# Two early weight blocks and an earlier residual in a two-block transformer kernel

## The chip, the cores and the metric

One core of a Trainium2 chip runs the kernel. TensorE (PE) multiplies, VectorE (DVE), ScalarE (ACT) and GpSimd (POOL) do the elementwise work, and SyncE (SP) issues most of the DMAs. The metric is the device time in microseconds of one execution, the median of several.

## The reference, cut to what matters

Two transformer blocks follow one another on 256 tokens of width 1024, in fp32. The first block (two layers, with attention, MLP and a final RMS norm) ends in `x`. The second block has two layers of its own, and each of them is this, with three attentions between (cut):

```python
for l in range(DEPTH):
    mod = jax.nn.silu(c) @ w_ada[l] + b_ada[l]
    shift, scale, gate = jnp.split(mod, 3, axis=-1)
    h = x * (1.0 + scale[:, None, :]) + shift[:, None, :]
    (p_cq, p_ckv, p_kr, p_qb, p_kb, p_vb, p_qc, p_kc, p_vc,
     p_qi, p_ki, p_wi, p_gate) = jnp.split(h @ w_in[l], SPLIT_POINTS, axis=-1)
    cq = rms_norm(p_cq, q_norm_g[l])        # 768 latents
    ckv = rms_norm(p_ckv, kv_norm_g[l])     # 256 latents
    ...
    sub = y @ w_out[l]
    x = layer_norm(ALPHA * x + (1.0 + gate[:, None, :]) * sub, ln_g[l], ln_b[l])
```

The term `ALPHA * x` is the residual that the change moves, and the 1024 latents are the columns whose weights it takes in early.

## The kernel before

The 256 tokens lie in two tiles of 128, "token 0" and "token 1" below (`t`). Every fp32 product is made of three matmuls: both factors are split into a rounded part (`whi`, `ahi`) and the rest (`wlo`, `alo`), and `mm3` (L330 to L332) adds hi x hi, lo x hi and hi x lo. Weights are streamed in blocks of 128 x 1024 by the class `Weights`, in the order of one list, `weight_plan`: SyncE loads a block into one of 4 raw buffers (L190, L194), ScalarE casts it to `whi` (L207), VectorE subtracts to `wlo` (L209). `get` hands out the next block of the list and keeps the split running two blocks ahead, in 5 buffers of each kind. `W.hold` ties later subtractions on VectorE behind a named instruction; `turn_input` sets it to the first alo.

The order on every engine is made by a scheduler from the program's order and its dependences. `tc.issue_after` adds an edge for instructions of the same engine.

The stages that the change touches:

- **End of the first block** (`mlp1`). The last four blocks (`m1w2`) give each token's sums; then per token come the RMS norm (L1238 to L1243, a pow on GpSimd in `rsqrt`, L340), two modulated halves (L1250), their transposes on TensorE (L1267), and the split of the transposed input into `ahi` (ScalarE, L1269) and `alo` (VectorE, L1270).
- **Entry of a layer of the second block** (`block2_layer`, `l` = 0 and 1). A loop takes steps for token 0, and three steps behind (`LAG`) the same steps for token 1. Its blocks are eight of the latents ("b2c", two halves of 512 columns with four blocks each), four of 392 columns ("b2vb") and two of 256 ("b2vc"). When a half is complete, VectorE multiplies it by the gains `lgain` (L1632), which SyncE loads (L1608, L1609). When both halves of a token are complete, `latent_scale` sums the squares, has GpSimd make the pow of two columns (L340), and scales the latents (L1645, L1646). Then they are transposed and split (L1667 to L1670).
- **The residual**, `resid`, ALPHA times the layer's input, needed at the layer's end. In layer 0 it is a product by a column (L1256) and one by a row (L1257) for each token, on GpSimd. In layer 1 it is two small products on GpSimd (L1881, L1882), a ScalarE activation (L1883), and two products or sums by a row on GpSimd (L1885), for each token.
- **End of a layer** (`out_tok`, `finish`): two halves of 512 columns for two tokens, with L1845 to L1847 on VectorE behind each, and for each token the layer norm (L1851 to L1859). Layer 0's end calls `turn_input` again; layer 1's stores the output (L1861).

Of the kernel before, what the change touches and what calls it, by code (L numbers as in the profile page):

```python
# [90 lines left out]
def weight_plan(A):  # L91
    plan = []

    def add(key, w, r0, nk, c0, nc_):
        plan.append((key, [(w[r0:r0 + 128 * nk, c0:c0 + nc_], 0, nc_)], nk, nc_))

    def group(key, w, c0, n=256):
        add(key + "0", w, 0, 4, c0, n)
        add(key + "1", w, 512, 4, c0, n)

    def mlp(l):
        w1, w2 = A["mlp_w1"][l], A["mlp_w2"][l]
        for e in range(9):
            if e < 8:
                for g in range(2):
                    group(f"m{l}w1", w1, e * 512 + g * 256)
            if e:
                for i in range(4):
                    if l:
                        add(f"m{l}w2", w2, e * 512 - 512 + 256 * (i // 2), 2, i % 2 * 512, 512)  # L110
                    else:
                        add(f"m{l}w2", w2, e * 512 - 512, 4, i * 256, 256)

    w = A["even_w_in"][0]
    for r0 in (0, 512):
        for c0 in (0, 256):
            add("l0in", w, r0, 4, c0, 256)
    for c0 in (512, 768, 1024, 1280):
        group("l0in", w, c0)
    w = A["even_w_out"][0]  # L120
    for kh in range(2):
        for g in range(4):
            add("l0out", w, kh * 512, 4, g * 256, 256)
    mlp(0)
    w = A["odd_w_in"][0]
    for kind, g in (("q", 0), ("q", 1), ("k", 0), ("v", 0), ("k", 1), ("v", 1),
                    ("q", 2), ("k", 2), ("v", 2), ("q", 3), ("k", 3), ("v", 3)):
        group("l1" + kind, w, {"q": 0, "k": 1024, "v": 2048}[kind] + g * 256)
    w = A["odd_w_out"][0]
    for kh in range(2):  # L130
        for g in range(4):
            add("l1out", w, kh * 512, 4, g * 256, 256)
    mlp(1)
    for l in range(2):
        w = A["w_in_2"][l]
        for g in range(2):
            for i in range(4):
                add("b2c", w, 256 * i, 2, 512 * g, 512)
        for i in range(4):
# [12 lines left out]
        for g in range(2):
            group("b2qi", w, 2976 + g * 256)
        one("b2qb", 1312)
        one("b2kb", 1696)
        add("b2uk", A["w_uk_2"][l], 0, 2, 0, 384)
        add("b2uv", A["w_uv_2"][l], 0, 2, 0, 384)
        for hh in range(2):
            for kq in range(3):

                r = A["w_uq_2"][l][256 * kq:256 * kq + 256, 288 * hh:288 * hh + 288]
                plan.append(("b2uq", [(r, a, n, c0) for a, n, c0 in ((0, 96, 0), (96, 16, 80), (112, 16, 64))], 2, 384))
        group("b2qc", w, 2208)
        group("b2kc", w, 2464)
        for g in (2, 1, 0, 3):
            group("b2g", w, 3560 + g * 256)
        for g in range(2):
            for i in range(4):
                add("b2o", A["w_out_2"][l], 256 * i, 2, 512 * g, 512)
    return plan  # L170


class Weights:
# [25 lines left out]
    def _split(self):  # L199
        i = self.i_split  # L200
        key, pieces, nk, n = self.plan[i]
        raw = self.raw.pop(i)
        hi = self.pool.tile([128, 1024], F32R, name="whi", tag="whi", bufs=self.bufs)
        lo = self.pool.tile([128, 1024], F32R, name="wlo", tag="wlo", bufs=self.bufs)
        m = nk * n
        with self.tc.issue_after(self.ahold) if self.ahold else contextlib.nullcontext():
            self.nc.scalar.copy(hi[:, :m], raw)  # L207
        with self.tc.issue_after(self.hold) if self.hold else contextlib.nullcontext():
            self.nc.vector.tensor_tensor(lo[:, :m], raw, hi[:, :m].bitcast(F32), op=OP.subtract)  # L209
        r = "p (k c) -> p k c"  # L210
        self.parts[i] = (hi[:, :m].rearrange(r, k=nk), lo[:, :m].rearrange(r, k=nk))
        self.i_split += 1
# [18 lines left out]
def cols(c, n=128):  # L231
    return slice(n * c, n * c + n)
# [48 lines left out]
class Net:  # L281
# [897 lines left out]
    def mlp1(self, a):  # L1179
# [25 lines left out]
        for e in range(8):  # L1205
# [16 lines left out]
            for i in range(4):  # L1222
                w = self.W.get("m1w2")
                for t in range(2):
                    product(e - 1, i, t, w)
            del hid[e - 1]
        ws = [self.W.get("m1w2") for _ in range(4)]
        hi4, lo4 = ([self.k4([128, 4, 256], F32R, name=n) for _ in range(2)] for n in ("ahi", "alo"))
        rstds = []
# [22 lines left out]
            rstds.append(rstd)  # L1252

        def resid(t, dep):
            with self.tc.issue_after(dep):
                nc.gpsimd.tensor_scalar(xt[t], xt[t], rstds[t], ALPHA, op0=OP.mult, op1=OP.mult)  # L1256
            nc.gpsimd.tensor_tensor(xt[t], xt[t], fr, op=OP.mult)  # L1257
            return xt[t]

# [2 lines left out]
    def turn_input(self, u, i, t, hi4, lo4):  # L1262

        nc = self.nc
        pt = self.psum("s" if i else "pt", [128, 4, 128])
        for k in range(4):
            nc.tensor.transpose(pt[:, k], u[:, cols(k)], self.ident)  # L1267
        hv, lv = (f[i][:, :, cols(t)] for f in (hi4, lo4))
        nc.scalar.copy(hv, pt)  # L1269
        op = nc.vector.tensor_tensor(lv, pt, hv.bitcast(F32), op=OP.subtract)  # L1270
        if i + t == 0:
            self.W.hold = op.ins


    def odd_q(self, wv, g, a):
# [324 lines left out]
    def block2_layer(self, l, a, resid):  # L1600
# [62 lines left out]
        for t in range(2):  # L1663
            for i in range(2):
# [3 lines left out]
                hv, lv = (f[i][:, :, cols(t)] for f in (chi4, clo4))  # L1668
                nc.scalar.copy(hv, pt)
                last = V.tensor_tensor(lv, pt, hv.bitcast(F32), op=OP.subtract)  # L1670
        xa = [resid(t, last.ins) for t in range(2)]
        last_lo = clo[7].bitcast(F32)


# [158 lines left out]
            hi4, lo4 = ([self.k4([128, 4, 256], F32R, name=n) for _ in range(2)] for n in ("ahi", "alo"))  # L1833
            hi, lo = ([t[:, i] for t in f for i in range(4)] for f in (hi4, lo4))
        mvs = []
        st = self.sb.tile([128, 2, 2, 6], F32, name="st", tag="st", bufs=1)

        def out_tok(g, t, ws):
            ps = self.psum("mm")
            for i, (wh, wl) in enumerate(ws):  # L1840
                for k in range(2):
                    kk = 2 * i + k
                    self.mm3(ps, (yh[kk][:, cols(t)], yl[kk][:, cols(t)]), (wh[:, k], wl[:, k]), kk == 0, kk == 7)
            c = cols(g, 512)
            V.tensor_tensor(z[t][:, c], ps, g1[:, c], op=OP.mult)  # L1845
            (V if g else nc.gpsimd).tensor_tensor(z[t][:, c], z[t][:, c], xa[t][:, c], op=OP.add)
            V.bn_stats(st[:, t, g], z[t][:, c])  # L1847

        def finish(t):
            mv = self.sm([128, 2])  # L1850
            V.bn_aggr(mv, st[:, t])  # L1851
            rstd = self.rsqrt(mv[:, 1:2], 1, 1.0, 1e-5, True)
            u = self.k4([128, 1024], name="u")
            for i in range(2):
# [9 lines left out]
            mvs.append((mv, rstd))  # L1864

        for g in range(2):
            ws = [self.W.get("b2o") for _ in range(4)]
            for t in range(2):
                out_tok(g, t, ws)
                if g:  # L1870
                    finish(t)
        if l == 1:
            return None, None
        def resid(t, dep):

            mv, rstd = mvs[t]
            r2, nb = self.sm([128, 1]), self.sm([128, 1])
            with self.tc.issue_after(dep):
                if t == 0:
                    nc.gpsimd.tensor_scalar(lnb, lnb, ALPHA, 0.0, op0=OP.mult, op1=OP.add)  # L1880
                nc.gpsimd.tensor_scalar(r2, rstd, ALPHA, 0.0, op0=OP.mult, op1=OP.add)  # L1881
            nc.gpsimd.tensor_scalar(nb, mv[:, 0:1], r2, -1.0, op0=OP.mult, op1=OP.mult)  # L1882
            nc.scalar.activation(z[t], z[t], AF.Identity, bias=nb, scale=r2)  # L1883
            for o, row in ((OP.mult, lng), (OP.add, lnb)):
                nc.gpsimd.tensor_tensor(z[t], z[t], row, op=o)  # L1885
            return z[t]
# [51 lines left out]
```

## Time and profile before

| | |
|---|---|
| Median of 3 runs | 1418.17 us (1415.57 to 1426.66) |
| The profiled execution | 1415.89 us |
| Its span, first to last instruction | 1414.1 us |
| Mean granted TensorE clock | 0.987 |
| Busy: TensorE, VectorE, ScalarE, GpSimd | 95%, 72%, 45%, 19% of the span |
| Chain that ended last: TensorE, VectorE, GpSimd, DMA | 15%, 4%, 1%, 1% of the span |

The times in the trace count from the first instruction. The first block ends, and the second block's layer 0 begins, at about 1035 us; layer 1 begins at about 1225 us. Busy shares are averages over the whole span; where an engine waits is seen in the rows of a stretch, each of which gives the idle time ahead of it in brackets and what ended it.

### The profile page before, as it was taken

The page shows a single profiled execution, that of the slowest core. Times are in us where ns is not written, and L with a number is a line of the kernel's source. Part 1 is how long each engine was busy: PE and PEld are TensorE (multiplying, and loading weights), DVE is VectorE, ACT ScalarE, POOL GpSimd, SP SyncE. Part 2 cuts the span into 40 slices and gives each one's busy share as a digit, 9 for nine tenths or more (in the row PEclk, how much of TensorE's full clock was granted, in tenths as well). Part 3 has the DMA queues.
Part 4 walks back from the last instruction along what each step waited for, and adds up shares of the span by engine and source line. Part 5 has one row for each costly group of instructions (what it writes and reads, how often), then busy time and mean ns, then how long its engine had stood idle before and what let it go on. Part 6 is the DMA issues. An engine that isn't in the chain of part 4 may idle for free. (4 is left out here: it accounts for less than half of the span.)

```text
span 1414.1 us, 23149 instructions
## 1 busy us (share of the span) xinstructions
PE 1344.2 (95%) x8747; PEld 1144.7 (81%) x8747; DVE 1016.7 (72%) x1885; ACT 637.5 (45%) x1225; POOL 271.8 (19%) x287
## 2 busy tenths in 40 slices
PE   6889999999999999999999999999989899999997
PEld 4666567898877887788898898989869789798896
DVE  4486676547778878897877776554576697777976
ACT  4354544433332223215555555444435456365562
POOL 0210000221110023144100013111131232141222
PEclk9999999999999999999999999999999999999999
DMA  9924553134669788982323226756647664566551
GB/s 292 313 71 165 180 173 115 31 105 134 196 194 314 245 269 277 305 266 64 105 62 104 75 83 200 222 179 193 186 123 230 155 180 157 172 166 184 141 185 45
DMA packets 213871, 242.23 MB, mean 171 GB/s; under 512 B 55903, under 2 KB 177792, under 8 KB 213760
## 3 DMA queue, kind: packets, MB, share of 16 engines
q1 hardware_dynamic: 203392, 236.82, 53.6%
q10 hardware_dynamic: 8576, 3.87, 1.0%
q8 instruction: 69, 1.13, 0.3%
q14 instruction: 42, 0.34, 0.1%
q0 software_dynamic: 1792, 0.06, 0.1%
HBM read 238.68 MB, written 2.03 MB: 170 GB/s over the span
## 5 line engine op out<-in xcount | busy, mean ns | idle before, releaser
L209 DVE TENSOR_TENSOR wlo<-raw,whi 128x1024 fp32r<-128x1024 f32 (+2 forms) x286 | 363.5, 1276 | 161.7 <-ACT whi L207 152.9
L207 ACT CAST whi<-raw 128x1024 fp32r<-128x1024 f32 (+2 forms) x286 | 292.4, 1030 | 308.7 <-PE mm L331 172.2
L330 PE MATMUL mm<-ahi,whi 128*128 128x256 f32 (+1 forms) x848 | 287.1, 339 | 0.0
L331 PE MATMUL mm<-alo,whi 128*128 128x256 f32 (+1 forms) x848 | 280.6, 331 | 0.0
L332 PE MATMUL mm<-ahi,wlo 128*128 128x256 f32 (+1 forms) x848 | 280.0, 330 | 0.0
L330 PEld LDWEIGHTS mm<-ahi,whi 128*128 128x128 f32 x848 | 162.3, 191 | 24.1 <-issue 7.1
L332 PEld LDWEIGHTS mm<-ahi,wlo 128*128 128x128 f32 x848 | 162.1, 191 | 15.8 <-issue 0.4
L331 PEld LDWEIGHTS mm<-alo,whi 128*128 128x128 f32 x848 | 162.1, 191 | 14.4 <-issue 0.7
L376 POOL TENSOR_TENSOR hid<-e,hid 128x512 fp32r<-128x512 f32 x48 | 77.1, 1607 | 357.2 <-ACT hid L375 314.4
L541 DVE SCALAR_TENSOR_TENSOR acc<-adaw,cst,acc 128x1024 f32<-128x1024 f32 x98 | 126.4, 1304 | 0.4
L330 PE MATMUL mm<-hid,whi 128*128 128x512 f32 (+1 forms) x288 | 106.7, 371 | 0.0
L331 PE MATMUL mm<-hid,whi 128*128 128x512 f32 (+1 forms) x288 | 105.9, 368 | 0.0
L332 PE MATMUL mm<-hid,wlo 128*128 128x512 f32 (+1 forms) x288 | 105.9, 368 | 0.0
L330 PE MATMUL s<-ahi,whi 128*128 128x256 f32 x256 | 72.9, 285 | 1.2 <-ACT ahi L377 1.2
L331 PE MATMUL s<-alo,whi 128*128 128x256 f32 x256 | 72.7, 285 | 0.1
L332 PE MATMUL s<-ahi,wlo 128*128 128x256 f32 x256 | 72.6, 284 | 0.0
L331 PE MATMUL mm<-wlo,ahi 128*128 128x256 f32 (+1 forms) x192 | 61.8, 323 | 3.4 <-DVE sm L338 3.4
L330 PE MATMUL mm<-whi,ahi 128*128 128x256 f32 (+1 forms) x192 | 63.3, 330 | 0.0
L330 PEld LDWEIGHTS mm<-hid,whi 128*128 128x128 f32 x288 | 54.1, 188 | 10.2 <-ACT whi L207 0.4
L332 PEld LDWEIGHTS mm<-hid,wlo 128*128 128x128 f32 x288 | 54.1, 188 | 9.7
L332 PE MATMUL mm<-whi,alo 128*128 128x256 f32 (+1 forms) x192 | 61.4, 322 | 0.5 <-DVE alo L1270 0.5
L331 PEld LDWEIGHTS mm<-hid,whi 128*128 128x128 f32 x288 | 54.2, 188 | 9.2
(361 smaller groups left out, 2807.2 us busy)
## 6 DMA issues: line engine op xcount, KB each, us to landing
raw<-in_mlp_w SPq DMA_DIRECT2D x128, 512.0 KB, 5.0
adaw<-in_ada_w SPq DMA_DIRECT2D x96, 512.0 KB, 5.6
raw<-in_w_in SPq DMA_DIRECT2D x64, 512.0 KB, 5.1
adaw<-in_w_ada SPq DMA_DIRECT2D x48, 512.0 KB, 5.7
raw<-in_odd_w_in SPq DMA_DIRECT2D x24, 512.0 KB, 4.2
raw<-in_w_out SPq DMA_DIRECT2D x16, 512.0 KB, 3.5
raw<-in_even_w_in SPq DMA_DIRECT2D x12, 512.0 KB, 5.9
raw<-in_even_w_out SPq DMA_DIRECT2D x8, 512.0 KB, 3.6
```

What stands on the lines that cost most here:

```text
L207: self.nc.scalar.copy(hi[:, :m], raw)
L209: self.nc.vector.tensor_tensor(lo[:, :m], raw, hi[:, :m].bitcast(F32), op=OP.subtract)
L330: mm(ps, w[0], x[0], start=start, stop=False, skip_group_check=skip)
L331: mm(ps, w[0], x[1], start=False, stop=False, skip_group_check=skip)
L332: mm(ps, w[1], x[0], start=False, stop=stop, skip_group_check=skip)
L376: return (lo_eng or nc.vector).tensor_tensor(lo, t, hf, op=OP.subtract)
L541: V.scalar_tensor_tensor(acc, raw, s, acc, op0=OP.mult, op1=OP.add)
```

## The change

It has four parts.

1. The first two latent blocks of layer 0 ("b2cx") stand in the plan, and are taken with `get`, ahead of the last four blocks of the first block's MLP; those of layer 1 ahead of the last four blocks of layer 0's output product. They have buffers of their own (2 of each kind).
2. `turn_input` no longer sets `W.hold`.
3. `resid` is called in the loop, at step LAG + 4, and tied by data to token 1's latents: a one-element copy from `lat[1]` into the small tile that the residual's first product writes. In layer 0 the product of `rstd` and ALPHA becomes a small instruction of its own.
4. In the last layer, the last half of token 1's output product is made in two parts of 256 columns.

```diff
+    EARLY = 2
...
+    def early(l):
+        for x in latents(l)[:EARLY]:
+            add("b2cx", *x)
...
+                    if l and e == 8 and i == 0:
+                        early(0)
...
+            if g and l == 0:
+                early(1)
...
-        hi = self.pool.tile([128, 1024], F32R, name="whi", tag="whi", bufs=self.bufs)
-        lo = self.pool.tile([128, 1024], F32R, name="wlo", tag="wlo", bufs=self.bufs)
+        x, bufs = ("x", 2) if key.endswith("x") else ("", self.bufs)
+        hi, lo = (self.pool.tile([128, 1024], F32R, name=n, tag=n + x, bufs=bufs) for n in ("whi", "wlo"))
...
+        self.early = [self.W.get("b2cx") for _ in range(2)]
         ws = [self.W.get("m1w2") for _ in range(4)]
...
         def resid(t, dep):
-            with self.tc.issue_after(dep):
-                nc.gpsimd.tensor_scalar(xt[t], xt[t], rstds[t], ALPHA, op0=OP.mult, op1=OP.mult)
+            r = self.sm([128, 1])
+            self.after(r, dep)
+            nc.gpsimd.tensor_scalar(r, rstds[t], ALPHA, 0.0, op0=OP.mult, op1=OP.add)
+            nc.gpsimd.tensor_scalar(xt[t], xt[t], r, 0.0, op0=OP.mult, op1=OP.add)
             nc.gpsimd.tensor_tensor(xt[t], xt[t], fr, op=OP.mult)
...
         op = nc.vector.tensor_tensor(lv, pt, hv.bitcast(F32), op=OP.subtract)
-        if i + t == 0:
-            self.W.hold = op.ins
...
             if i >= LAG:
                 token_step(i - LAG, 1, ws.pop(i - LAG))
+            if i == LAG + 4:
+                xa = [resid(t, lat[1]) for t in range(2)]
             for t in range(2):
                 if i - LAG * t == 7:
                     latent_scale(t)
...
-        xa = [resid(t, last.ins) for t in range(2)]
...
+            halves = 2 if l and g and t else 1
+            n = 512 // halves
+            for h in range(halves):
+                ps = self.psum("mm", [128, n])
...
             r2, nb = self.sm([128, 1]), self.sm([128, 1])
-            with self.tc.issue_after(dep):
-                if t == 0:
-                    nc.gpsimd.tensor_scalar(lnb, lnb, ALPHA, 0.0, op0=OP.mult, op1=OP.add)
-                nc.gpsimd.tensor_scalar(r2, rstd, ALPHA, 0.0, op0=OP.mult, op1=OP.add)
+            self.after(r2, dep)
+            if t == 0:
+                nc.gpsimd.tensor_scalar(lnb, lnb, ALPHA, 0.0, op0=OP.mult, op1=OP.add)
+            nc.gpsimd.tensor_scalar(r2, rstd, ALPHA, 0.0, op0=OP.mult, op1=OP.add)
```

Line numbers of the changed kernel differ: L338/L340 become L351/L353, L209 L222, L1250 L1264, L1256/L1257 L1272/L1273, L1270 L1286, L1632 L1646, L1645/L1646 L1659/L1660, L1881/L1882/L1883/L1885 L1903/L1904/L1905/L1907.

GpSimd, from token 0's first pow at the end of `mlp1` to the pow of two columns of layer 0's `latent_scale`, before:

```order
L340 TENSOR_TENSOR sm<-sm,cst 128x1
L1256 TENSOR_SCALAR xt<-xt,sm 128x1024
L1257 TENSOR_TENSOR xt<-xt,rows 128x1024
L368 COPY lgain<-ahi 1x1
L340 TENSOR_TENSOR sm<-sm,cst 128x1
L1256 TENSOR_SCALAR xt<-xt,sm 128x1024
L1257 TENSOR_TENSOR xt<-xt,rows 128x1024
L340 TENSOR_TENSOR sm<-sm,cst 128x2 x2
```

and after:

```order
L353 TENSOR_TENSOR sm<-sm,cst 128x1
L381 COPY lgain<-ahi 1x1
L353 TENSOR_TENSOR sm<-sm,cst 128x1
L381 COPY sm<-lat 1x1 x2
L1271 TENSOR_SCALAR sm<-sm 128x1 x2
L1272 TENSOR_SCALAR xt<-xt,sm 128x1024 x2
L1273 TENSOR_TENSOR xt<-xt,rows 128x1024 x2
L353 TENSOR_TENSOR sm<-sm,cst 128x2 x2
```

The residual's products moved from beside the two one-column pows to a place behind the second of them, ahead of both pows of two columns.

GpSimd at the entry of layer 1, from the pow of the first layer norm on, before:

```order
L340 TENSOR_TENSOR sm<-sm,cst 128x1
L340 TENSOR_TENSOR sm<-sm,cst 128x2 x2
L1881 TENSOR_SCALAR sm<-sm 128x1
L1882 TENSOR_SCALAR sm<-sm 128x1
L1881 TENSOR_SCALAR sm<-sm 128x1
L1882 TENSOR_SCALAR sm<-sm 128x1
L1885 TENSOR_TENSOR z<-z,rows 128x1024 x4
```

and after:

```order
L353 TENSOR_TENSOR sm<-sm,cst 128x1
L381 COPY sm<-lat 1x1
L1903 TENSOR_SCALAR sm<-sm 128x1
L1904 TENSOR_SCALAR sm<-sm 128x1
L381 COPY sm<-lat 1x1
L1903 TENSOR_SCALAR sm<-sm 128x1
L1904 TENSOR_SCALAR sm<-sm 128x1
L1907 TENSOR_TENSOR z<-z,rows 128x1024 x4
L353 TENSOR_TENSOR sm<-sm,cst 128x2 x2
```

Here too both pows of two columns now come behind all the residual's products.

VectorE at the entry of layer 0, from token 0's modulated halves to those of token 1, before:

```order
L1250 SCALAR_TENSOR_TENSOR z<-z,sm,rows 128x512 x2
L1270 TENSOR_TENSOR alo<-pt,ahi 128x4x128
L209 TENSOR_TENSOR wlo<-raw,whi 128x1024
L1270 TENSOR_TENSOR alo<-s,ahi 128x4x128
L1238 TENSOR_TENSOR z<-mm,rows 128x512 x2
L1239 TENSOR_TENSOR xt<-z,xt 128x512 x2
L1247 TENSOR_TENSOR z<-xt,rows 128x512 x2
L1243 TENSOR_TENSOR sm<-sm 128x1
L209 TENSOR_TENSOR wlo<-raw,whi 128x1024
L338 TENSOR_SCALAR sm<-sm 128x1
L209 TENSOR_TENSOR wlo<-raw,whi 128x1024
L1250 SCALAR_TENSOR_TENSOR z<-z,sm,rows 128x512 x2
```

and after:

```order
L1264 SCALAR_TENSOR_TENSOR z<-z,sm,rows 128x512 x2
L222 TENSOR_TENSOR wlo<-raw,whi 128x1024
L1286 TENSOR_TENSOR alo<-pt,ahi 128x4x128
L222 TENSOR_TENSOR wlo<-raw,whi 128x1024
L1286 TENSOR_TENSOR alo<-s,ahi 128x4x128
L1252 TENSOR_TENSOR z<-mm,rows 128x512 x2
L1253 TENSOR_TENSOR xt<-z,xt 128x512 x2
L1261 TENSOR_TENSOR z<-xt,rows 128x512 x2
L1257 TENSOR_TENSOR sm<-sm 128x1
L1646 TENSOR_TENSOR lat<-mm,lgain 128x512
L351 TENSOR_SCALAR sm<-sm 128x1
L222 TENSOR_TENSOR wlo<-raw,whi 128x1024
```

A subtraction moved ahead of token 0's first alo, one ahead of token 1's pow request (L338, now L351) went, and token 0's first latents (L1646) now come ahead of that request.

## Rows read from the trace of the kernel before

**Rows 1.** Timeline of TensorE from 1030 us: start, us, instruction, [idle before <-releaser].

```profile
1044.58 0.80 PE L331 MATMUL mm<-wlo,ahi 128*128 128x512 f32 x1 [3.37 <-DVE sm L338]
...
1074.94 0.39 PE L331 MATMUL s<-wlo,ahi 128*128 128x256 f32 x1 [0.71 <-DVE wlo L209]
...
1104.91 0.88 PE L1574 MATMUL pt<-cst,e 128*128 128x128 f32 x3 [5.00 <-DVE e L1564]
...
1288.17 0.93 PE L1552 MATMUL s<-qkb 64*128 64x128 f32 x8 [2.06 <-ACT qkb L1728]
```

**Rows 2.** Windows: PE, PEld, DVE, ACT, POOL busy; PEclk, DMA share, GB/s.

```profile
1040.00:1050.00 10.00, 6.03 (x24) 4.13 (x23) 9.37 (x15) 2.71 (x7) 5.15 (x3) 0.83 0.82 236
...
1100.00:1110.00 10.00, 5.09 (x26) 3.81 (x27) 7.97 (x26) 4.75 (x14) 3.53 (x3) 0.66 0.85 260
...
1044.00:1044.50 0.50, 0.00 (x0) 0.00 (x0) 0.50 (x2) 0.00 (x0) 0.00 (x0) 0.67 0.18 39
1044.50:1045.00 0.50, 0.42 (x1) 0.42 (x2) 0.50 (x3) 0.00 (x0) 0.33 (x1) 0.50 0.00 0
```

**Rows 3.** Timelines of VectorE and GpSimd at the entry of layer 0.

```profile
1033.51 2.28 DVE L1250 SCALAR_TENSOR_TENSOR z<-z,sm,rows 128x512 f32<-128x512 f32 x2 [0.68 <-POOL sm L340]
...
1036.31 2.81 DVE L209 TENSOR_TENSOR wlo<-raw,whi 128x1024 fp32r<-128x1024 f32 x1
...
1044.45 0.14 DVE L338 TENSOR_SCALAR sm<-sm 128x1 f32<-128x1 f32 x1
...
1046.18 2.28 DVE L1250 SCALAR_TENSOR_TENSOR z<-z,sm,rows 128x512 f32<-128x512 f32 x2 [0.46 <-POOL sm L340]
...
1033.58 1.67 POOL L1256 TENSOR_SCALAR xt<-xt,sm 128x1024 f32<-128x1024 f32 x1
1035.34 2.70 POOL L1257 TENSOR_TENSOR xt<-xt,rows 128x1024 f32<-128x1024 f32 x1
```

**Rows 4.** Timeline of VectorE at the entry of layer 1.

```profile
1228.74 1.21 DVE L209 TENSOR_TENSOR wlo<-raw,whi 128x1024 fp32r<-128x1024 f32 x1
...
1231.14 1.40 DVE L1856 SCALAR_TENSOR_TENSOR u<-z,sm,rows 128x512 f32<-128x512 f32 x2
```

**Rows 5.** Timelines of VectorE, GpSimd and TensorE, latents of layer 0.

```profile
1058.89 0.69 DVE L1632 TENSOR_TENSOR lat<-mm,lgain 128x512 f32<-128x512 f32 x1 [0.44 <-PE mm L332]
...
1065.62 0.97 DVE L209 TENSOR_TENSOR wlo<-raw,whi 128x784 fp32r<-128x784 f32 x1
...
1064.08 0.71 POOL L340 TENSOR_TENSOR sm<-sm,cst 128x2 f32<-128x2 f32 x1 [13.36 <-DVE sm L338]
...
1066.65 0.45 PE L331 MATMUL s<-wlo,ahi 128*128 128x392 f32 x1
```

**Rows 6.** Timeline of SyncE's queue at the entry of layer 0.

```profile
1039.59 0.47 SPq L1608 DMA_DIRECT2D lgain<-in_q_norm_g  x1
```

**Rows 7.** Timelines of VectorE, GpSimd, ScalarE and TensorE, latents of layer 1.

```profile
1244.73 0.69 DVE L1632 TENSOR_TENSOR lat<-mm,lgain 128x512 f32<-128x512 f32 x1 [1.73 <-PE mm L332]
...
1261.03 6.27 DVE L209 TENSOR_TENSOR wlo<-raw,whi 128x1024 fp32r<-128x1024 f32 x2 [0.97 <-ACT whi L207]
...
1258.27 0.52 POOL L1882 TENSOR_SCALAR sm<-sm 128x1 f32<-128x1 f32 x1
...
1260.43 12.50 POOL L1885 TENSOR_TENSOR z<-z,rows 128x1024 f32<-128x1024 f32 x4
...
1258.82 1.24 ACT L1883 ACTIVATE z<-z,sm 128x1024 f32<-128x1024 f32 x1 [1.02 <-POOL sm L1882]
...
1254.83 0.34 PE L331 MATMUL s<-wlo,ahi 128*128 128x392 f32 x1
```

**Rows 8.** Timeline of GpSimd in layer 0, 1092 to 1106 us.

```profile
1092.78 2.38 POOL L1681 TENSOR_TENSOR tmp<-rows 128x1024 f32<-128x1024 f32 x1 [7.14 <-DMA rows<-row]
...
1095.49 1.04 POOL L1880 TENSOR_SCALAR rows<-rows 128x1024 f32<-128x1024 f32 x1
```

**Rows 9.** Timeline of VectorE at the end of the kernel.

```profile
1403.38 1.41 DVE L1859 SCALAR_TENSOR_TENSOR u<-u,sm,rows 128x512 f32<-128x512 f32 x2
```

More of the change, by code (lines that the diff above doesn't have):

```diff
@@ L99, in group, with latents @@
         add(key + "1", w, 512, 4, c0, n)
+    EARLY = 2
+    def latents(l):
+        return [(A["w_in_2"][l], 256 * i, 2, 512 * g, 512) for g in range(2) for i in range(4)]
+    def early(l):
+        for x in latents(l)[:EARLY]:
+            add("b2cx", *x)
     def mlp(l):
@@ L135, in weight_plan @@
         w = A["w_in_2"][l]
-        for g in range(2):
-            for i in range(4):
-                add("b2c", w, 256 * i, 2, 512 * g, 512)
+        for x in latents(l)[EARLY:]:
+            add("b2c", *x)
         for i in range(4):
@@ L1652, in block2_layer @@
             if i < len(steps):
-                ws[i] = self.W.get(("b2c", "b2c", "b2vb", "b2vc")[steps[i][0]])
+                ws[i] = self.early.pop(0) if self.early else self.W.get(("b2c", "b2c", "b2vb", "b2vc")[steps[i][0]])
                 token_step(i, 0, ws[i])
@@ L1835, in block2_layer @@
         mvs = []
-        st = self.sb.tile([128, 2, 2, 6], F32, name="st", tag="st", bufs=1)
+        st = self.sb.tile([128, 2, 3, 6], F32, name="st", tag="st", bufs=1)
         def out_tok(g, t, ws):
[L1839 to L1847, printed above, removed]
+            halves = 2 if l and g and t else 1
+            n = 512 // halves
+            for h in range(halves):
+                ps = self.psum("mm", [128, n])
+                for i, (wh, wl) in enumerate(ws):
+                    for k in range(2):
+                        kk = 2 * i + k
+                        self.mm3(ps, (yh[kk][:, cols(t)], yl[kk][:, cols(t)]), (wh[:, k, cols(h, n)], wl[:, k, cols(h, n)]),
+                                 kk == 0, kk == 7)
+                c = slice(512 * g + n * h, 512 * g + n * h + n)
+                V.tensor_tensor(z[t][:, c], ps, g1[:, c], op=OP.mult)
+                (V if g else nc.gpsimd).tensor_tensor(z[t][:, c], z[t][:, c], xa[t][:, c], op=OP.add)
+                V.bn_stats(st[:, t, g + h], z[t][:, c])
         def finish(t):
             mv = self.sm([128, 2])
-            V.bn_aggr(mv, st[:, t])
+            V.bn_aggr(mv, st[:, t, 0:3 if l and t else 2])
             rstd = self.rsqrt(mv[:, 1:2], 1, 1.0, 1e-5, True)
@@ L1866, in block2_layer @@
         for g in range(2):
+            if g and l == 0:
+                self.early = [self.W.get("b2cx") for _ in range(2)]
             ws = [self.W.get("b2o") for _ in range(4)]
```

## The prediction

> **What bounds the kernel now.** I read the page first: TensorE is busy for nearly the whole span, so a change can win at most the places where TensorE waits, and can lose wherever it makes TensorE wait anew. Next I listed TensorE's idle times from 1000 us on, where the change acts, each with what ended it. Three are above 2 us and lie in the stages touched: 3.37 us at the entry of the second block's layer 0, 5.00 us at a softmax inside it, 2.06 us in layer 1 [rows 1]. The windows show a second price: the granted clock reads 0.83 over 1040 to 1050, round the idle of 3.37 us, and 0.66 over 1100 to 1110, round the one of 5.00 us; right behind the first, over 1044.5 to 1045, it is 0.50, the lower of its two levels (1.2 in place of 2.4 GHz) [rows 2]. A window of 10 us at 0.83 holds 3.4 us of that level. Some 4 us of work at half speed is 2 us lost, if TensorE is the bound behind the idle.
>
> **Entry of layer 0 (early blocks, no residual on GpSimd there, no hold).** Token 0's residual runs on GpSimd from 1033.58 to 1038, and VectorE's work beside it stretches: the pair L1250 takes 2.28 us and a weight subtraction 2.81 us [rows 3], where the same kinds (L1856, L209) take 1.40 and 1.21 us with GpSimd idle [rows 4]. Moving the residual away gives VectorE back 0.88 + 1.60 us; one more subtraction of 1.21 now stands ahead of the first alo, so token 1's chain begins 1.3 us earlier. Its request for the pow, L338 at 1044.45 [rows 3], has one subtraction less ahead of it but gets token 0's latent row, the new L1646 (old L1632, 0.69 us [rows 5]), which needs lgain. With lgain in time, the request comes at 1044.45 - 1.3 - 1.2 + 0.7 = 1042.6. From there to the last two z, L1250, it took 1.73 us (to 1046.18), or some 0.9 with a pow of 0.71 us as in layer 0 [rows 5]; these two take 1.40 and end at 44.9 to 45.7 instead of 1046.18 + 2.28 = 1048.46 [rows 3]: 2.7 to 3.6 us won. lgain is the doubt. In SyncE's order its loads stand behind two more weight loads, each of which needs a raw buffer that a subtraction must free. Before, it was issued at 1039.59 [rows 6], and the DMA share fell to 0.18 in the window 1044.0 to 1044.5 [rows 2], where I put its landing. Issued an us earlier or at the same time, it lands at 43 to 44.5 against a wish at 42; at the late end the chain wins next to nothing. TensorE gets all of token 0's three lead steps done early now, and then idles for token 1 in one piece of about 3 us, so the slow clock may fall on work that bounds: 0 to 1.7 us lost, where it lay on lead steps before. Bounds -3.6 and +2.0; lgain one us late (-2.1) and 1.2 us for the clock give **-0.9 us**.
>
> **Layer 0's residual in front of the pow.** GpSimd's order now has two copies, two small products, two tensor_scalars and two tensor_tensors, all released by the first half of token 1's latents, and behind them the pow of token 0's latents. The release is 1058.89 + 0.69 = 1059.58 [rows 5]. The four small ones take up to 0.52 each (L1882 [rows 7]); the tensor_scalar 1.04 us alone [rows 8], 1.67 beside VectorE [rows 3]; the tensor_tensor 2.38 alone [rows 8], 2.70 beside VectorE [rows 3]. Sum: 0..2.1 + 2.1..3.3 + 4.8..5.4, 6.9 to 10.8. The pow, at 1064.08 before [rows 5], starts at 1066.5 to 1070.4: +2.4 to +6.3 us. On VectorE the latents' scaling waits for it, and the subtractions of b2vb's third and fourth block are queued behind that. The first of them was ready at 1065.62 + 0.97 = 1066.59 and TensorE used it at 1066.65 [rows 5]: no slack, so TensorE waits all of that, in one piece. I take 4.3, since VectorE has work in half of that time. Such an idle lies between the two that cost the clock: 1.8 us more (0 at the low end); the idle of 0.71 us at 1074.94 [rows 1] is absorbed. **+5.4 us** (1.7 to 7.4).
>
> The Trainium skill (page "SBUF — State Buffer", section "Who interferes with whom") says that a VectorE instruction with two SBUF inputs and a GpSimd instruction that reads SBUF lock each other out, the second to issue waiting until the first ends; its summary advises to schedule whichever is off the critical path. The trace agrees: the subtraction of 2.81 us lies beside L1257's 2.70 [rows 3]. It speaks against putting long GpSimd reads ahead of a step that TensorE waits for, and with full lockout the dear ends of this term and of layer 1's would hold: +15 in all.
>
> **Entry of layer 1.** No residual ran here, so nothing is given back. One more subtraction (1.21 us, L209 [rows 4]) stands between token 1's first gate product and token 0's alo, while one ahead of token 1's alo, partly hidden by ScalarE's cast, goes. Token 1's chain is about an us longer and TensorE has hardly an idle here to absorb it: **+1.0 us** (0 to 1.2).
>
> **Layer 1's residual in front of the pow.** The release is 1244.73 + 0.69 = 1245.42 [rows 7]. A copy and two small products (0 to 1.6 us), then ScalarE's L1883, 1.24 us [rows 7], which it now runs ahead of a weight cast of b2vb's second block; the first product L1885 starts at 1246.7 to 1248.2. Four of them take 4 x 2.38 = 9.5 us alone [rows 8] or 12.50 beside VectorE's subtractions, as measured [rows 7]. From the pow's start to the end of the subtraction behind it layer 0 took 1066.59 - 1064.08 = 2.5 us [rows 5]. Block 4 is ready at 1258.7 to 1263.2; TensorE used it at 1254.83 [rows 7]: +3.9 to +8.4, I take the middle, 6.2. This wait comes in two or more pieces (the delayed cast gives the first), so for the clock I take 1.0 (0 to 1.8). Given back: the residual no longer stretches subtractions (two to 6.27 us [rows 7]) from 1261 on, which through late raw buffers, a late load and its cast ends in TensorE's idle of 2.06 us [rows 1]: -2.1. **+5.1 us** (1.8 to 8.1).
>
> **The last product in halves.** Half of the rows L1845 to L1847 could go ahead of TensorE's last matmuls, but VectorE is busy with token 0's L1859 until 1404.79 [rows 9], some 0.2 us before it starts on token 1, and three more instructions cost something: **+0.2 us** (-0.1 to +0.4).
>
> **Sum.** -0.9 + 5.4 + 1.0 + 5.1 + 0.2 = +10.8 us on the profiled execution's own 1415.89: 1426.7. That execution is 2.3 us under the median of the runs shown (1418.17; 1415.57 to 1426.66), so the forecast is **1429.0 us**. All low ends together give -0.3, all high ends +19.1: 1417.9 to 1437.3.
>
> **Rivals.** *Faster:* the early blocks do what they are for and the residual is hidden. It is decided at the pow of token 0's latents in layer 0: if GpSimd gets through its eight instructions between 1059.58 and 1064.08, in 4.5 us, nothing waits, and in layer 1 likewise. Then the entry's 2.7 us and the 2.1 us at 1288 remain: 1418.17 - 4.8 = 1413.4. Against it: the two tensor_tensors alone take 4.8 us, and the four in layer 1 9.5. Chance 0.10. *Half hidden:* GpSimd runs at its undisturbed durations, because the subtractions that would collide are themselves held up behind the pow; the clock holds, since each wait stays under 3.37 us; and lgain lands in time. That is the sum of low ends, -0.3, to about +5: 1421. Chance 0.17. *Dearer still:* both pows at their dear ends (+2.0, +2.2), the clock in full at all three places (+1.3), and two more subtractions colliding at 6.27 / 2 - 1.21 = 1.9 us each: 10.8 + 9.3 = +20.1, 1438.3. Chance 0.09. That the change doesn't do what it says concerns the early blocks: TensorE's idle at the entry ends with token 1's chain and not with weights, so that weights are there early wins nothing by itself; this is inside the first term.
>
> **How the numbers follow.** My sum has 0.64. The range reaches from 1414.5 (three single runs of one kernel lie from 2.6 us below to 8.5 above their median, and so the faster rival is partly in) to 1439. A change within 1% (14.2 us: 1404 to 1432.4) is about what a measurement of this kernel cannot tell from none. Of my main case nearly four in ten lie above 1432.4, and all of the dearer one: slower 0.34. Faster by over 1% needs more than the idles of this stage give: 0.04. The same: 0.62.
>
> **What would show it.** In the profile of the changed kernel: the pair L1264 (the old L1250) near 1.4 us and no subtraction of 2.8 us at the entry; the pow L353 on two columns 2 to 6 us later in layer 0, counted from the first half of token 1's latents, and 8 to 12 us later in layer 1; behind each a new idle of TensorE released by a weight subtraction; no idle of 2 us at layer 1's first scores. I am wrong if the pow runs ahead of the products, if TensorE has other matmuls ready there, or if lgain alone holds token 1 at the entry.

## The result, and the profile after

The changed kernel takes 1424.79 us (median of 20 runs, 1421.0 to 1428.46), the kernel before 1415.66 us beside it (20 runs, 1410.55 to 1426.66): 9.1 us or 0.61% slower, ratio 1.0061, 95% interval 1.0049 to 1.0074. The forecast was +10.8 us on a median of 1418.17, which later runs of the same kernel put 2.5 us lower. The measured 1424.79 us lies in the stated range of 1414.5 to 1439, and the change is within 1%.

The profiled execution has a span of 1426.0 us, 11.9 more than before. The page says little of the cause: TensorE is busy for the same 95%, with 12.7 us more. The mean clock of 0.979 against 0.987 says nothing of the change: 84 other executions of the kernel before show 0.976 to 0.985, so it is the profiled execution of the kernel before that stands out.

```profile
PE 1356.9 (95%) x8771; PEld 1155.5 (81%) x8771; DVE 1017.5 (71%) x1888; ACT 638.3 (45%) x1225; POOL 270.1 (19%) x293
```

TensorE's timeline of the changed kernel, with the idle ahead of each row and what ended it, answers to [rows 1]; L344 is the old L331, L1588 the old L1574:

```profile
1048.23 1.11 PE L1283 MATMUL pt<-cst,z 128*128 128x128 f32 x4 [4.33 <-DVE z L1264]
...
1068.29 0.45 PE L344 MATMUL s<-wlo,ahi 128*128 128x392 f32 x1 [2.14 <-DVE sm L1656]
1073.12 0.44 PE L344 MATMUL s<-wlo,ahi 128*128 128x392 f32 x1 [0.55 <-DVE wlo L222]
...
1109.91 0.88 PE L1588 MATMUL pt<-cst,e 128*128 128x128 f32 x3 [3.50 <-DVE e L1578]
...
1208.64 0.50 PE L343 MATMUL mm<-whi,yh 128*128 128x512 f32 x1 [1.59 <-ACT yh L388]
1210.18 0.50 PE L345 MATMUL mm<-whi,yl 128*128 128x512 f32 x1 [0.80 <-POOL yl L389]
...
1235.41 0.50 PE L345 MATMUL mm<-whi,alo 128*128 128x512 f32 x1 [0.86 <-DVE alo L1286]
1241.76 0.66 PE L1283 MATMUL pt<-cst,u 128*128 128x128 f32 x4 [1.00 <-DVE u L1879]
...
1260.12 0.46 PE L344 MATMUL s<-wlo,ahi 128*128 128x392 f32 x1 [0.55 <-DVE wlo L222]
1265.58 0.44 PE L344 MATMUL s<-wlo,ahi 128*128 128x392 f32 x1 [3.18 <-DVE wlo L222]
1270.28 0.45 PE L344 MATMUL s<-wlo,ahi 128*128 128x392 f32 x1 [0.70 <-DVE wlo L222]
```

New waits stand at the b2vb blocks of both layers, and at yh and yl; the idle of 2.06 us at layer 1's first scores is gone. To size them I took each matmul's start in both timelines and subtracted: the lateness. The matmul at 1066.65 of [rows 5] starts at 1073.12 now, 6.47 us late; the one at 1254.83 of [rows 7] at 1270.28, 15.45 us late. Where lateness jumps, time was lost. A change of lateness holds the idles and the slow clock of both executions, so differences of some 1.7 us between single executions are not the kernel's for certain (the last section works the number out). By stages:

| stretch | lateness from, to | change |
|---|---|---|
| entry of layer 0, to the fourth block | 1.76, 1.86 | +0.1 |
| latents of layer 0 | 1.86, 6.47 | +4.6 |
| first softmax, ropes of layer 0 | 6.47, 4.95 | -1.5 |
| yh, yl ahead of layer 0's output product | 4.95, 7.30 | +2.35 |
| entry of layer 1 | 7.30, 8.40 | +1.1 |
| latents of layer 1 | 8.40, 15.45 | +7.05 |
| first scores and ropes of layer 1 | 15.45, 11.96 | -3.5 |
| the end | 11.96, 11.88 | -0.1 |

The 1.76 us at the start were there before the change acts: single executions drift against each other, by -5.4 to +1.5 us at 980 us in the profiles of this study. The rest is +10.1.

VectorE and GpSimd at the entry and in the latents of layer 0, after, which answer to [rows 3] and [rows 5]:

```profile
1035.41 1.41 DVE L1264 SCALAR_TENSOR_TENSOR z<-z,sm,rows 128x512 f32<-128x512 f32 x2 [0.68 <-POOL sm L353]
1036.74 1.22 DVE L222 TENSOR_TENSOR wlo<-raw,whi 128x1024 fp32r<-128x1024 f32 x1
...
1045.09 0.69 DVE L1646 TENSOR_TENSOR lat<-mm,lgain 128x512 f32<-128x512 f32 x1 [1.13 <-DMA lgain<-in_q_norm_g]
...
1060.77 0.69 DVE L1646 TENSOR_TENSOR lat<-mm,lgain 128x512 f32<-128x512 f32 x1 [1.72 <-PE mm L345]
...
1065.23 3.00 DVE L222 TENSOR_TENSOR wlo<-raw,whi 128x784 fp32r<-128x784 f32 x1 [0.17 <-ACT whi L220]
...
1068.16 0.14 DVE L1656 TENSOR_SCALAR sm<-sm 128x1 f32<-128x1 f32 x1
1068.33 2.15 DVE L351 TENSOR_SCALAR sm<-sm 128x2 f32<-128x2 f32 x1
1071.31 0.62 DVE L1659 TENSOR_SCALAR lat<-lat,sm 128x768 f32<-128x768 f32 x1 [0.82 <-POOL sm L353]
...
1062.83 2.24 POOL L1272 TENSOR_SCALAR xt<-xt,sm 128x1024 f32<-128x1024 f32 x2
1065.03 5.43 POOL L1273 TENSOR_TENSOR xt<-xt,rows 128x1024 f32<-128x1024 f32 x2
1070.57 0.70 POOL L353 TENSOR_TENSOR sm<-sm,cst 128x2 f32<-128x2 f32 x1
```

The pair L1264 takes 1.41 us and the subtraction 1.22, as forecast, and lgain comes 1.13 us late. The pow starts 1070.57 - 1061.46 = 9.1 us after token 1's first half, before 4.5. The same rows show a second effect: the request for the pow, L351, two columns wide, takes 2.15 us, and a subtraction 3.00, while L1273 runs. (This holding up of VectorE while GpSimd works is called lockout below.) In layer 1 the four L1907 take 10.94 us, and two instructions of one or two columns about 2 us each. The pow starts 1267.71 - 1253.82 = 13.9 us after token 1's first half (L1646, which ends at 1253.82), before 4.2, so 9.7 us later:

```profile
1259.99 2.35 DVE L1655 TENSOR_TENSOR sm<-sm 128x1 f32<-128x1 f32 x1
...
1262.70 1.95 DVE L351 TENSOR_SCALAR sm<-sm 128x2 f32<-128x2 f32 x1
...
1256.81 10.94 POOL L1907 TENSOR_TENSOR z<-z,rows 128x1024 f32<-128x1024 f32 x4 [0.61 <-ACT z L1905]
1267.71 0.71 POOL L353 TENSOR_TENSOR sm<-sm,cst 128x2 f32<-128x2 f32 x1
```

### The profile page after: what moved, and what is told of

Same layout as the page of the kernel before. It is cut to its first block, busy times and chain, and to the rows that moved or that the text cites. A ratio compares the mean times of both kernels' runs of the same rounds, so it can differ in the third digit from the quotient of the medians.

```text
span 1426.0 us, 23230 instructions
## 1 busy us (share of the span) xinstructions
PE 1356.9 (95%) x8771; PEld 1155.5 (81%) x8771; DVE 1017.5 (71%) x1888; ACT 638.3 (45%) x1225; POOL 270.1 (19%) x293
## 3 DMA queue, kind: packets, MB, share of 16 engines
q8 instruction: 69, 1.13, 0.3%
## 4 chain that ended last, share of the span: by engine, by line
PE 76%; DVE 10%; DMA 4%; issue 3%; POOL 3%; ACT 2%; SPq 1%; ACTq 0%; DVEq 0%; POOLq 0%
PE mm L343 18%; PE mm L344 18%; PE mm L345 18%; PE s L344 3%; PE s L345 3%; PE s L343 3%; DMA adaw<-in_ada_w 2%; PE om L1097 2%; DVE wlo L222 2%; PE pt L1082 2%; PE mm L522 1%; PE s L1031 1%; PE om L1433 1%; PE s L1566 1%; DMA rpbs<-rpb 1%
## 5 line engine op out<-in xcount | busy, mean ns | idle before, releaser
L222 DVE TENSOR_TENSOR wlo<-raw,whi 128x1024 fp32r<-128x1024 f32 (+2 forms) x286 | 358.0, 1257 | 164.4 <-ACT whi L220 154.1
L220 ACT CAST whi<-raw 128x1024 fp32r<-128x1024 f32 (+2 forms) x286 | 293.3, 1030 | 323.5 <-PE mm L344 158.5
L344 PE MATMUL mm<-alo,whi 128*128 128x256 f32 (+1 forms) x848 | 281.0, 331 | 0.0
L344 PEld LDWEIGHTS mm<-alo,whi 128*128 128x128 f32 x848 | 162.5, 192 | 14.6 <-issue 0.7
L344 PE MATMUL mm<-hid,whi 128*128 128x512 f32 (+1 forms) x288 | 106.0, 368 | 0.0
L344 PE MATMUL s<-alo,whi 128*128 128x256 f32 x256 | 72.8, 285 | 0.1
L344 PE MATMUL mm<-wlo,ahi 128*128 128x256 f32 (+1 forms) x192 | 62.5, 325 | 0.0
L344 PEld LDWEIGHTS mm<-hid,whi 128*128 128x128 f32 x288 | 54.2, 188 | 9.2
```

The costliest lines, as they stand in the source:

```text
L344: mm(ps, w[0], x[1], start=False, stop=False, skip_group_check=skip)
```

## The experiments

Each was timed over five rounds beside the kernel before. The theory to begin with: the loss comes from GpSimd's queue, in which the pow stands behind the residual. The rivals: the early blocks are the cost, or GpSimd's reads lock VectorE out wherever they stand.

**Early blocks alone**: plan, `get` and the lost hold as in the change, the residual as before.

> Early blocks and no hold, the residual where it was before, no halving at the end. Queue theory (the loss comes from the pow of the latents standing behind the residual on GpSimd): against the kernel before +2 to +5 us, from a later yh at layer 0's end (+2.4, half of it absorbed), layer 1's entry (+1.1) and a slow clock at layer 0's entry; no TensorE idle above 1 us at the b2vb blocks. Rival (the early blocks and the lost hold are the cost, by pushing four blocks' splits back): +8 to +9 us, the whole loss.

1422.94 against 1417.0 us, ratio 1.0043 (1.0026 to 1.0061): +6 us, somewhat over the theory's band, short of the rival's. No idle of 0.5 us or more stands at the b2vb blocks. TensorE's timeline shows 2.50 us of idle that I had not expected, at layer 0's entry, and the wait for yh:

```profile
1037.38 0.50 PE L345 MATMUL mm<-whi,alo 128*128 128x512 f32 x1 [2.50 <-DVE alo L1284]
1047.54 0.66 PE L1281 MATMUL pt<-cst,z 128*128 128x128 f32 x4 [3.24 <-DVE z L1264]
...
1207.72 0.50 PE L343 MATMUL mm<-whi,yh 128*128 128x512 f32 x1 [1.48 <-ACT yh L388]
```

**The residual alone**: the reverse.

```diff
+            if i == LAG + 4:
+                xa = [resid(t, lat[1]) for t in range(2)]
...
-        xa = [resid(t, last.ins) for t in range(2)]
```

> Only the residual's new place, the plan and the hold as before. Queue theory: -1 to -2.7 us at layer 0's entry, +4.6 and +7.0 us at the two pows, -2.1 and -1 given back: +4 to +9 us against the kernel before, with TensorE idle behind a weight subtraction at the b2vb blocks of both layers. Rival (early blocks are the cost): 0 to -3 us.

1428.73 against 1417.0, ratio 1.0081 (1.0058 to 1.0104): +11.5 us, above the theory's band, and the rival is out. The entry of layer 0 wins 1.2 us in lateness, so the residual's place alone carries the whole loss. The idle in layer 0 is one piece here, and the slow clock follows it (0.66 over 1068 to 1078); another slow stretch follows a rope's wait (0.66 over 1160 to 1170):

```profile
1069.81 0.70 PE L331 MATMUL s<-wlo,ahi 128*128 128x392 f32 x1 [4.30 <-DVE wlo L209]
...
1161.01 2.50 PE L1554 MATMUL s<-ka,qa 96*128 96x128 f32 x6 [2.43 <-POOL qa L1900]
```

The two parts' losses, 6 and 11.5, don't add up to the change's 9.1. In the profiled executions part of it is that without the residual at the entry the lost hold costs less there: the entry of layer 0 adds 3.9 us of lateness with the early blocks alone, and 0.1 in the changed kernel. The rope's wait and slow stretch above make up most of the rest, and the changed kernel has 0.90 us of idle there.

**The residual after the loop**, in the changed kernel: both pows stand ahead of it.

```diff
-            if i == LAG + 4:
-                xa = [resid(t, lat[1]) for t in range(2)]
...
                 if i - LAG * t == 7:
                     latent_scale(t)
+        xa = [resid(t, lat[1]) for t in range(2)]
```

> The changed kernel with the residual called after the token loop, so that both pows of two columns stand ahead of it on GpSimd. Queue theory: the 4.6 and 7.0 us go, some 3 us that were given back return: -1 to +2 us against the kernel before, no idle above 1 us at the b2vb blocks. Rival (GpSimd's long reads lock VectorE out wherever they stand near the latents): +6 us or more.

1427.95 against 1417.0, ratio 1.0076 (1.0052 to 1.0100). The times agree with the lockout rival, and yet the trace has no idle above 0.3 us at the b2vb blocks of either layer. The loss stands elsewhere, at the first softmax of layer 0. TensorE, ScalarE and GpSimd:

```profile
1110.92 0.88 PE L1588 MATMUL pt<-cst,e 128*128 128x128 f32 x3 [10.66 <-DVE e L1578]
...
1084.10 0.48 ACT L1640 COPY vabc<-s 128x384 f32<-128x384 f32 x1 [6.26 <-POOL xt L1273]
...
1078.37 5.70 POOL L1273 TENSOR_TENSOR xt<-xt,rows 128x1024 f32<-128x1024 f32 x2
```

ScalarE waits 6.26 us to the very end of the residual. The row `fr` that L1273 reads lies in a rotating buffer, and token 1's `vabc` takes that buffer next.

**The pow on VectorE**: in the changed kernel, `latent_scale` makes its root by Newton steps, `rsqrt(s[:, 0:2], 2, 1.0 / 768, 1e-6)`.

> The changed kernel with the latents' inverse root made on VectorE by Newton steps (some 14 small instructions of 0.15 us, 2 us a token) instead of a pow on GpSimd; the residual stays where the change put it. Queue theory: VectorE no longer waits for GpSimd's queue, the idle at the b2vb blocks falls to 2 us or less in each layer, +2 to +5 us against the kernel before. Rival (lockout): the small instructions are held one by one between GpSimd's reads, the idle stays at 4 us or more in each layer: +8 us or more.

1428.28 against 1417.0, ratio 1.0082 (1.0060 to 1.0104): the lockout rival's number. The idle is 4.14 us in layer 0, with no pow in GpSimd's queue. TensorE and VectorE:

```profile
1070.29 0.49 PE L344 MATMUL s<-wlo,ahi 128*128 128x392 f32 x1 [4.14 <-DVE wlo L222]
...
1063.44 2.19 DVE L357 TENSOR_SCALAR sm<-sm 128x2 f32<-128x2 f32 x1
1065.67 2.27 DVE L359 TENSOR_SCALAR sm<-sm 128x2 int32<-128x2 int32 x1
```

The first two of the small instructions take 2.2 us each, beside L1273; the later ones, with GpSimd idle, 0.15. The two are 4.2 us longer than that, which is the idle. In layer 1 the idle is 5.54 us, ended by a subtraction that L1907 stretches to 3.09 us. So the queue was half the story: where the residual stands, lockout alone gives a wait as long.

**`fr` in a buffer of its own**, with the late residual:

```diff
+                fr = self.sb.tile([128, 1024], F32, name="fr", tag="fr", bufs=1)
```

> The changed kernel with the residual after the token loop (as in the run with the late residual) and the row fr in a buffer of its own. Buffer theory (the late residual holds fr, whose buffer token 1's vabc takes next, so that ScalarE's queue stops for 6.26 us and all behind it, up to the first softmax of layer 0, is 5.7 us late): that idle of 10.66 us falls back to about 5, and the kernel stands +4 to +6 us over the one before, which is what the early blocks alone cost. Rival (GpSimd's reads beside VectorE's subtractions make the same delay): idle still 9 us or more, +9 us or more.

1423.21 against 1415.86, ratio 1.0051 (1.0033 to 1.0069). By the medians this is +7.4 us, between the two bands. The idle falls from 10.66 to 7.69 us, not to 5: the buffer was 3 us of it.

```profile
1106.63 0.87 PE L1592 MATMUL pt<-cst,e 128*128 128x128 f32 x3 [7.69 <-DVE e L1582]
```

The times alone don't tell this kernel from the one with the late residual.

**The late residual without early blocks**, `fr` in its own buffer, the hold kept.

> The kernel before with the late residual and fr in its own buffer, without early blocks and with the hold. Queue and buffer theory: the entry of layer 0 keeps its gain of about 1.5 us, no pow stands behind the residual, nothing else moves: -3 to 0 us against the kernel before. Rival (lockout beside the subtractions wherever the residual stands): +3 us or more.

1416.95 against 1415.86, ratio 1.0008 (0.9989 to 1.0026): the same; the interval, -1.6 to +3.7 us, reaches into both bands. The loss of the change is undone by undoing the residual's place and the early blocks, but nothing is won: the entry gains 1.2 us, and 2.6 us are lost at the first softmax (7.64 us of idle where 5.00 stood). GpSimd's residual stretches three subtractions to 7.53 us, clo comes later, so do the rows' loads, and the tables behind them. TensorE, VectorE, GpSimd:

```profile
1102.24 0.87 PE L1580 MATMUL pt<-cst,e 128*128 128x128 f32 x3 [7.64 <-DVE e L1570]
...
1074.48 7.53 DVE L209 TENSOR_TENSOR wlo<-raw,whi 128x1024 fp32r<-128x1024 f32 x3 [0.21 <-ACT whi L207]
...
1095.16 0.29 DVE L1562 CUSTOM_DVE_ANT_0 e<-s,bb 128x128 f32<-128x128 f32 x1 [6.05 <-DMA bb<-in_k_bias]
...
1090.17 2.39 POOL L1687 TENSOR_TENSOR tmp<-rows 128x1024 f32<-128x1024 f32 x1 [6.25 <-DMA rows<-row]
1092.51 0.41 POOL L368 COPY bb<-qkb 1x1 f32<-1x1 f32 x3
```

This suggests what the idle of 5.00 us of [rows 1] is: the copies that release the tables `bb` stand on GpSimd behind a product that waits for rows. In the kernel before, the two products behind those copies add to it: a subtraction that stands between the first head's two softmax rows on VectorE takes 4.28 us beside them.

```profile
1098.03 4.28 DVE L209 TENSOR_TENSOR wlo<-raw,whi 128x1024 fp32r<-128x1024 f32 x1
...
1096.51 2.40 POOL L1682 TENSOR_TENSOR rows<-rows 128x1024 f32<-128x1024 f32 x1
1098.88 2.35 POOL L1683 TENSOR_TENSOR rows<-tmp,rows 128x1024 f32<-128x1024 f32 x1
```

The next run moves all three products, so it shows that they are the cause together, and not what the late tables and the held subtraction cost each.

**The rows' products later**: the kernel before, with only these three instructions moved behind the fifth table.

```diff
-            nc.gpsimd.tensor_tensor(tmp, lnb, gr, op=OP.mult)
-            nc.gpsimd.tensor_tensor(gr, lng, gr, op=OP.mult)
-            nc.gpsimd.tensor_tensor(sr, tmp, sr, op=OP.add)
...
             nc.sync.dma_start(b, A["k_bias"][h])
+            if h == 4 and l == 0:
+                nc.gpsimd.tensor_tensor(tmp, lnb, gr, op=OP.mult)
+                nc.gpsimd.tensor_tensor(gr, lng, gr, op=OP.mult)
+                nc.gpsimd.tensor_tensor(sr, tmp, sr, op=OP.add)
```

> The kernel before with one thing moved: the three products of rows L1681 to L1683 on GpSimd, which wait for rows and stand ahead of the copies that release the tables bb of the first softmax, come after the fifth table instead. Theory (layer 0's idle of 5.00 us at the first softmax comes from GpSimd's queue: tables late, and VectorE locked out by L1682 and L1683): that idle falls below 2 us and the slow clock behind it goes, -4 to -7 us. Rival (the softmax waits for its scores): within 1 us of before.

1408.56 against 1415.86, ratio 0.9942 (0.9921 to 0.9963): 7.3 us faster by the medians, faster than both kernels. The idle is gone (so the softmax did not wait for its scores), the windows show the full clock where [rows 2] had 0.66, and the first softmax starts at 1089.96. Part comes back at a rope. Windows, VectorE, TensorE:

```profile
1100.00:1110.00 10.00, 10.00 (x86) 9.40 (x87) 7.84 (x22) 5.77 (x14) 0.00 (x0) 1.00 0.67 148
...
1089.96 0.29 DVE L1556 CUSTOM_DVE_ANT_0 e<-s,bb 128x128 f32<-128x128 f32 x1 [1.76 <-PE s L1552]
...
1136.61 0.49 PE L1552 MATMUL s<-ka,qa 96*128 96x128 f32 x2 [3.10 <-POOL qa L1898]
```

**Both**: late residual, no early blocks, and the rows' products later.

> Both: the late residual with fr in its own buffer, no early blocks, and the rows' products after the fifth table. If the gains add up: -5 to -9 us against the kernel before. Rival (one of the two gains is absorbed by the next wait, in layer 0's rope at 1154 us): -3 to -5 us.

1416.71 against 1415.86, ratio 1.0004 (0.9990 to 1.0019): a miss for both. The rope isn't what takes the gain back: its idle is 3.12 us here and 3.10 in the kernel with the rows' products later alone. The gain is gone before it. From 1090 to 1111 us of the kernel before, that one wins 7.2 us of lateness, and this one loses 0.6: in place of the 5.00 us it idles for 3.40 us ahead of the scores that need a copy of `qkb` by ScalarE, and the clock is 0.66 over 1097 to 1107. The copy stands behind the second head's softmax, whose rows come 6.6 us behind the first head's on VectorE (L1562, the old L1556), with a subtraction, L1756, another subtraction and L1902 between; with the rows' products later alone the two come within 1 us. TensorE and VectorE:

```profile
1096.80 0.49 PE L1558 MATMUL s<-qkb 64*128 64x128 f32 x4 [3.40 <-ACT qkb L1731]
...
1088.54 0.29 DVE L1562 CUSTOM_DVE_ANT_0 e<-s,bb 128x128 f32<-128x128 f32 x1 [3.08 <-PE mm L332]
...
1095.17 0.29 DVE L1562 CUSTOM_DVE_ANT_0 e<-s,bb 128x128 f32<-128x128 f32 x1 [0.95 <-POOL misc L1904]
```

Why the scheduler puts VectorE's rows in this order with the late residual is open.

**Early blocks for layer 0 only**, in the changed kernel.

> The changed kernel with early blocks for layer 0 only; layer 1's eight latent blocks stand in the plan where they stood before. Theory (layer 1's two early blocks put weight casts and subtractions ahead of the last yh and yl of layer 0 and of the alo at layer 1's entry): TensorE's idles of 1.59 and 0.80 us before L0's output product go, with the slow clock behind them, and of the 1.1 us at layer 1's entry about one: -3 to -4.5 us against the changed kernel, +4.5 to +6 over the one before. Rival (the yh wait comes from work that the residual's delay shifted): as the changed kernel, +9 us.

1426.06 against 1416.56, ratio 1.0072 (1.0048 to 1.0095): as the changed kernel, so the expected -3 to -4.5 us is a miss in time. In the trace the wait for yh is gone (0.28 us is left at yl, at 1209.71), so that layer 1's early blocks cause it is shown; but layer 0's idle is one piece of 4.31 us here, and a rope's wait with a slow stretch costs 2.8 us that the changed kernel didn't lose. The wait of 1.03 us at layer 1's entry is still there.

**The halves alone.**

> The kernel before with the last product in two halves and nothing else. Prediction's term: +0.2 us (-0.1 to +0.4), not to be told from none by the times, but to be read in the trace as the time from the last product's first matmul to the last instruction. Rival (the halves let VectorE's three rows begin earlier): -0.5 us or more.

1418.53 against 1416.56, ratio 1.0006 (0.9986 to 1.0026). From VectorE's row L1845 (old lines) of token 0's last half to token 1's first output DMA: 1399.56 to 1409.60 before, 10.04 us; 1398.99 to 1408.93 here, 9.94. That is -0.1 us, at the edge of the term's bounds, and not the rival's -0.5.

**The rows' products behind the third table.**

> The kernel before with the three products of rows after the third table instead of the fifth. Theory (any place behind the copies for bb frees the first softmax; at the fifth table they delay the ropes by the 2.4 us that came back at 1142 us there): -8 to -11 us against the kernel before. Rival (here they lock VectorE out beside the second pair's softmax): -3 to -6 us.

1408.7 against 1416.56, ratio 0.9950 (0.9931 to 0.9970): 7.9 us faster, not to be told from the fifth table.

**Without the hold.** The kernel before, less the two lines that set it.

> The kernel before without the hold, and nothing else. If the extra subtractions ahead of the alo at layer 1's entry (1 us, still there with early blocks for layer 0 only) come from the lost hold: +1 us in the trace at layer 1's entry and a later token 1 chain at layer 0's entry by up to a subtraction, 1.2 us; in the times 0 to +3 us, hardly to be told from none. Rival (it comes from early blocks): no shift at layer 1's entry.

1420.29 against 1418.86, ratio 1.0015 (0.9994 to 1.0037). In the trace the waits at layer 1's entry are there (0.94 and 0.98 us) without any early block, so they come from the lost hold. At layer 0's entry the hold was worth more than I had thought:

```profile
1035.57 0.79 PE L332 MATMUL mm<-whi,alo 128*128 128x512 f32 x1 [2.49 <-DVE alo L1270]
```

## Why the prediction was right, step by step

- **Entry of layer 0**, forecast -0.9, measured +0.1. VectorE's rows shrank as told and lgain was late by 1.13 us, near the one us taken. The idle for token 1 is 4.33 us in one piece. The term isn't settled by this pair of executions: three others whose code is the kernel before's up to here (the halves alone, and the rows' products later in both places) lose 1.6 us of lateness at this entry against the profiled execution of the kernel before, with a clock of 0.66 over 1040 to 1050 where [rows 2] has 0.83. Against them the changed kernel wins 1.5 us. The halves alone:

```profile
1040.00:1050.00 10.00, 7.40 (x23) 5.40 (x24) 7.41 (x11) 2.89 (x7) 5.84 (x3) 0.66 0.49 156
```

  What I left out: the lost hold puts subtractions ahead of alo, which costs 2.5 us of idle where the residual still stands there. In the changed kernel this idle is 0.27 us.
- **Latents of layer 0**, forecast +5.4, measured +4.6, and the pow's own delay 9.1 - 4.5 = 4.6 against 4.3. The sizes hold; that TensorE waits in one piece, and the step that added 1.8 us of clock on top, are wrong for this kernel. TensorE stopped early, at block 2 (2.14 us), because a subtraction there took 3.00 us, and its slow stretch (0.66 over 1068 to 1073) lies inside the wait for the pow. Where the idle is in one piece (the residual alone), the clock's loss comes on top, as told, and that kernel is dearer.
- **The mechanism of that wait** is told too narrowly. The forecast has the pow behind the residual in a queue. With no pow on GpSimd the idle is 4.14 us all the same: lockout of VectorE is a second sufficient cause. What is shown is that the residual's place causes it (it goes with the residual after the loop); queue and lockout stand side by side. In layer 0 they end together: the pow's request L351 ends at 1070.48 and the residual's last product at 1070.46. In layer 1 the queue ends last: the request ends at 1264.65, and the pow waits until the fourth L1907 ends at 1267.75. There lockout still gives the largest idle, 3.18 us, since the subtraction that ends it stands on VectorE behind L1655 and L351. The forecast let lockout stretch subtractions only, and had no price for small instructions.
- **Entry of layer 1**, forecast +1.0, measured +1.1; the cause is the lost hold (shown by its removal alone), not the early blocks.
- **Latents of layer 1**, forecast +6.2 and 1.0 for the clock, measured +7.05: 4.8 us of idle and a slow clock (0.66 over 1266 to 1271), again inside the wait. The pow came 9.7 us later, within the 8 to 12 told. For the -2.1 us at layer 1's first scores -2.4 was measured (lateness 15.45 to 13.04). That idle is gone in the four kernels with the residual in the loop; in the ten that have it elsewhere, the kernel before with its 2.06 among them, it reads 0 to 2.06 us, in six of them 0.9 to 1.3. So about half of this gain belongs to the one profiled execution of the kernel before, and not to the change.
- **The halves**, forecast +0.2, measured -0.1.
- **Not foreseen**: yh and yl, +2.35 us. Layer 1's early blocks put casts and subtractions ahead of layer 0's last gate, in a stage that I did not look at, since the order had moved little there. It was paid by idles in layer 0 that absorbed 1.5 us and by another 1.1 at layer 1's ropes.
- **Two slips in the sums**: the low ends add up to -0.2 us, not -0.3. And that a change within 1% can hardly be told from none was too cautious: 0.61% was measured to 0.13% either way.

The stages that the forecast has terms for come to +10.35 in this pair of executions, against +10.8. What it doesn't have nearly cancels: +2.35 at yh against -1.5 and -1.1 absorbed. Within the terms, layer 0's entry (+1.0 over the forecast) and its latents (-0.8) cancel too. That much is luck. The place of the loss at the two pows, and the size of their delays, are not.

## What to carry to other kernels

Work on GpSimd that is taken off the critical path must go where the critical path doesn't need VectorE beside it: look not only at the queue it joins but at the VectorE instructions that run beside it, the small ones too, and at the rotating buffers its operands hold longer. Data that arrive early win nothing where a chain of another engine ends the wait, and their casts and subtractions displace others in the stage that they are moved into. The gain in this kernel lay in an idle that the trace had shown all along (5.00 us behind a softmax): following it back to a copy queued behind an unrelated product gave 7 us with three instructions moved.

## What the runs showed of the hardware that was not expected

A GpSimd operation on 128 x 1024 held up VectorE instructions of one or two columns until it ended: 2.15 us for L351 (0.17 alone), a tensor_scalar on two columns, and 2.35 for L1655 (0.15 alone), a tensor_tensor on one. Not all of them: L1656, a tensor_scalar on one column, took 0.14 and 0.15 us beside L1273 and L1907. The Trainium skill ("SBUF — State Buffer", section "Who interferes with whom") says that tensor_scalar in a two-port mode contends with GpSimd; the rows agree for L351, down to two columns, though none shows its mode.

The granted clock isn't settled by the length of an idle alone. The kernel with halves and the one before are the same at the rope, with 2.00 us of idle in both, and over the next 10 us one shows 0.83 and the other 1.00:

```profile
1153.34 1.35 PE L1552 MATMUL s<-ka,qa 96*128 96x128 f32 x6 [2.00 <-POOL qa L1902]
...
1152.00:1162.00 10.00, 8.66 (x60) 7.95 (x61) 9.80 (x35) 3.76 (x12) 2.84 (x4) 0.83 0.55 166
```

```profile
1154.62 1.35 PE L1552 MATMUL s<-ka,qa 96*128 96x128 f32 x6 [2.00 <-POOL qa L1897]
...
1154.00:1164.00 10.00, 9.38 (x79) 8.82 (x80) 9.85 (x34) 4.52 (x12) 2.72 (x4) 1.00 0.52 153
```

A mean of 0.83 over 10 us is 1.7 us of full-speed work lost, so a single profile can't tell effects of that size.
